# Seven block products per pair of heads in another order, with 21 between u and q and the banks exchanged from pair to pair

## The chip, the cores and the metric

One core of one Trainium2 chip runs the whole program in one launch. The metric is device time in microseconds (us), the median over the runs of a kernel; lower is better. The engines are called as the profile calls them: PE (matrix multiply), DVE (vector), ACT (scalar), POOL (GpSimd), SP (the queue that issues most transfers).

## What is computed

A decoder block on 512 tokens of width 2048, in float32. One projection gives the inputs of two groups of attention heads and their gates z:

```python
h = _rmsnorm(x, norm_g[l])
proj = h @ w_in[l]
(qa, kca, vca, ksa, vsa, kwa, vwa, za, ga,
 qb, kb, vb, zb) = jnp.split(proj, offsets, axis=-1)
...
y_a = o_a.reshape(B, S, WIDTH_A) * jax.nn.silu(za)   # 8 heads of 128: compressed, selected and window attention
...
y_b = o_b.reshape(B, S, WIDTH_B) * jax.nn.silu(zb)   # 16 heads of 64: window of 128 with sinks
x = x + jnp.concatenate([y_a, y_b], axis=-1) @ w_out[l]
return _rmsnorm(x, final_g)
```

Queries are turned by a rotary embedding (rope: products with a sine and a cosine table and a sum) before their scores.

## The kernel before

**Arithmetic.** A float32 factor is split into a high and a low word of a shorter format, and a product is the sum of three matmuls (`mm3`): L127 high·high, L128 high weight·low activation, L129 low weight·high activation. The splitting of a weight tile of 128 × 1024 is a *unit*: ACT copies the high word (L641, `whi`), DVE subtracts it from the raw tile (L642, `wlo`). The words lie in a pool of three buffers, so a unit can be built only when the product three units earlier has ended.

**A pair.** Heads go through the program one by one ("pairs" h = 1 to 14, the pair being a head's 128 columns of q and of z, where for group B one such head stands for two of the 64-wide ones). For a pair, q and z over the two halves of the tokens (H0 and H1, 256 columns each), summed over even and odd blocks of the inner dimension, form a 2 × 2 block product, done with seven products and sums before and after them (Strassen–Winograd). They have names:

- p (on the stored activation sums `pu00`, `pu10`), 22, 12, 21 and w on slices of the activations `xh`, `xl`, u on `pu01`, `pu11`, and q on further sums that lie in the rooms of `VH`, `VL`, `KH`, `KL`;
- each is 24 matmuls of 256 columns, so a pair has 168 and the fourteen have 98 products;
- weights come by `load` (SP, 512 KB each) from four quarters; the units of w, u and q are sums of quarters that DVE makes (L699, `raw`). Pairs h > 9 ("wide") have five buffers and let an accumulating transfer on POOL's queue make some of the sums.

The code is `pair` (from L681); the order of the products in it is 22, p, 21, 12, w, u, q. Two PSUM banks `pa`, `pb` (both named `pj`) take them by halves: `pa` holds p and 12 in its first half and w in its second; `pb` holds 22 and 21 in the first and u and q in the second. Between products DVE (`plus`, L699) and ACT (L731, L742, L747 and the like) carry the results to the rows of q (tile `t1`, shown as t; in wide pairs also `dd`) and of z (`zr`). When u has been read, q's rows are complete: the sine (L760, twice), the cosine (L761) on DVE, the sum on POOL (L762), then the split of the query.

**Attention.** Group A (`attn_a`, after each of the pairs h = 1 to 7 and once before) makes scores for four blocks of queries, "score sets" of 3, 6, 6 and 9 matmuls (L565) into one buffer `sp`, which DVE empties (L567, L571) before the next set; then exponentials on ACT, transposes on PE (L603, L615, L617) with their split (L533 on ACT, L534 on DVE), and the products with the values (L609 to L611, L624, L626). Group B (`attention`) runs in the following pair: scores S (L903, L904, two sets of 8 matmuls for each of the parts s0 and s1), transposes L936, values L942, L943, L948. Its query tile `qs` is put together by two ACT copies (L870), a DVE subtraction `qlo` (L873) and four transfers of 64 KB on SP's queue (L882).

**What sets the order.** The program is written as one stream; a scheduler with a model of the engines' times orders the instructions of each engine when the program is built, by priority in the order of the code and by readiness. The order on every engine is then fixed. For group B, `hooks` (L965 and following) says behind which product of the next pair a piece of attention is issued: s0 behind 21, s1 behind 12, k0 behind w, k2 and k3 behind u, k1 and the end behind q.

## Time and profile before

| | us |
|---|---|
| median of 3 runs | 834.11 (831.44 to 838.43) |
| the profiled execution | 830.96 |
| its span | 829.1 |
| PE busy in it | 796.3 (96%) |
| PE's weight loads (PEld) | 746.1 (90%) |
| DVE busy | 688.4 (83%) |
| ACT busy | 521.9 (63%) |
| POOL busy | 91.3 (11%) |
| mean granted clock of PE | 0.996 |

The pairs with attention A run from about 210 to 489 us, those with attention B from there to about 640; what precedes is the normalisation, the keys, values and compressed keys, what follows is head 15 and the output projection. A row of the timeline gives the start in us, the duration, the engine, the line, output<-inputs, and in brackets how long the engine stood idle before it and what ended that. A row of waits gives the engine with the waiting line and, behind the arrow, what ended the wait: the us in total, how often, the longest. A row of windows gives the stretch, its length, the busy time of PE, PEld, DVE, ACT and POOL with the count of instructions, the granted clock, the busy share of the transfer engines and GB/s.

### The profile page before, as it was taken

How to read it: one execution, taken by the hardware profiler on the slowest of the kernel's cores; microseconds unless marked ns; L12 is line 12 of the kernel's file. 1: busy time of each engine (PE TensorE's matmuls, PEld its weight loads, DVE VectorE, ACT ScalarE, POOL GpSimd, SP SyncE). 2: the span in 40 equal slices, each digit the busy share in tenths (PEclk: the TensorE clock that was granted, in tenths of full speed). 3: DMA queues.
4: the chain of work that ended last, by engine and by line, in shares of the span. 5: the costliest groups of instructions: out<-in, count | busy, mean ns of one | idle time of the engine just before them, and what ended most of it. 6: DMA issues, size and time to landing. Idle time of an engine off the chain costs nothing.

```text
span 829.1 us, 15441 instructions
## 1 busy us (share of the span) xinstructions
PE 796.3 (96%) x5782; PEld 746.1 (90%) x5782; DVE 688.4 (83%) x1283; ACT 521.9 (63%) x1088; POOL 91.3 (11%) x75
## 2 busy tenths in 40 slices
PE   8999999999999999999999999999999998899996
PEld 7788898988999999999999899899988887899996
DVE  6869785975798989997997898889987998678894
ACT  6734456662577867866777478676875657443545
POOL 3510002022010011010110012101110000100000
PEclk9999999999999999999999999999999999999999
DMA  8665886899712215323213585666674236697835
GB/s 308 210 204 166 277 283 209 250 307 359 251 44 95 77 42 165 109 61 113 85 58 115 159 205 153 168 174 153 179 261 158 77 102 245 189 262 192 267 66 203
DMA packets 60475, 145.03 MB, mean 175 GB/s; under 512 B 6257, under 2 KB 19825, under 8 KB 60401
## 3 DMA queue, kind: packets, MB, share of 16 engines
q1 hardware_dynamic: 56944, 132.00, 48.2%
q0 software_dynamic: 3168, 11.54, 8.2%
q8 instruction: 45, 0.74, 0.4%
q10 hardware_dynamic: 288, 0.52, 0.2%
q14 instruction: 30, 0.24, 0.1%
HBM read 121.65 MB, written 20.55 MB: 172 GB/s over the span
## 4 chain that ended last, share of the span: by engine, by line
PE 69%; DVE 10%; DMA 10%; ACT 4%; issue 4%; SPq 1%; POOL 1%; ACTq 0%; DVEq 0%; POOLq 0%
PE pj L127 12%; PE pj L129 12%; PE pj L128 12%; PE bank L129 4%; PE bank L128 3%; PE bank L127 3%; PE sp L565 3%; PE oa L128 3%; PE oa L129 3%; PE oa L127 3%; DMA rw<-wos 2%; DMA qs<-qlo 2%; DMA raw<-wq 1%; DVE wlo L642 1%; DMA ch<-wos 1%
## 5 line engine op out<-in xcount | busy, mean ns | idle before, releaser
L127 PE MATMUL pj<-xh,whi 128*128 128x256 f32 (+1 forms) x560 | 170.7, 305 | 2.7 <-ACT whi L641 1.5
L129 PE MATMUL pj<-xh,wlo 128*128 128x256 f32 (+1 forms) x560 | 170.1, 304 | 3.0 <-DVE wlo L642 2.9
L128 PE MATMUL pj<-xl,whi 128*128 128x256 f32 (+1 forms) x560 | 169.0, 302 | 0.0
L641 ACT ACTIVATE whi<-raw 128x1024 fp32r<-128x1024 f32 x98 | 102.8, 1054 | 46.7 <-PE pj L128 19.4
L642 DVE TENSOR_TENSOR wlo<-raw,whi 128x1024 fp32r<-128x1024 f32 x98 | 122.0, 1249 | 8.8 <-ACT whi L641 8.4
L129 PEld LDWEIGHTS pj<-xh,wlo 128*128 128x128 f32 x560 | 105.5, 188 | 8.9 <-DVE wlo L642 4.0
L127 PEld LDWEIGHTS pj<-xh,whi 128*128 128x128 f32 x560 | 105.5, 188 | 8.5 <-ACT whi L641 1.9
L128 PEld LDWEIGHTS pj<-xl,whi 128*128 128x128 f32 x560 | 105.4, 188 | 4.4 <-issue 0.2
L97 DVE TENSOR_TENSOR wlo<-raw,whi 128x512 fp32r<-128x512 f32 (+2 forms) x74 | 80.7, 1095 | 33.8 <-ACT whi L96 33.6
L96 ACT ACTIVATE whi<-raw 128x1024 fp32r<-128x1024 f32 (+1 forms) x73 | 65.3, 900 | 57.9 <-PE pj L128 14.9
L127 PE MATMUL pj<-pu,whi 128*128 128x256 f32 x224 | 63.9, 285 | 0.4 <-DVE zr L699 0.3
L129 PE MATMUL pj<-pu,wlo 128*128 128x256 f32 x224 | 63.4, 283 | 0.0
L128 PE MATMUL pj<-pu,whi 128*128 128x256 f32 x224 | 63.2, 282 | 0.0
L699 DVE TENSOR_TENSOR raw<-raw 128x1024 f32<-128x1024 f32 x46 | 58.0, 1261 | 0.2
L762 POOL TENSOR_TENSOR t<-t,t 128x512 f32<-128x512 f32 x14 | 24.4, 1745 | 248.1 <-DVE sums L584 79.6
L128 PE MATMUL oa<-wlo,xh 128*128 128x256 f32 (+1 forms) x168 | 50.3, 299 | 1.5 <-DVE wlo L1016 0.9
L127 PE MATMUL oa<-whi,xh 128*128 128x256 f32 (+1 forms) x168 | 50.0, 300 | 0.9 <-ACT whi L1015 0.9
L129 PE MATMUL oa<-whi,xl 128*128 128x256 f32 (+1 forms) x168 | 50.0, 299 | 0.0
L127 PEld LDWEIGHTS pj<-pu,whi 128*128 128x128 f32 x224 | 42.2, 189 | 1.4 <-DVE zr L699 1.3
L533 ACT ACTIVATE ph<-tp 128x512 fp32r<-128x512 f32 x56 | 32.1, 590 | 16.9 <-PE tp L936 8.6
L129 PEld LDWEIGHTS pj<-pu,wlo 128*128 128x128 f32 x224 | 42.3, 189 | 0.5 <-DVE wlo L642 0.2
L128 PEld LDWEIGHTS pj<-pu,whi 128*128 128x128 f32 x224 | 42.2, 188 | 0.1
(364 smaller groups left out, 2347.0 us busy)
## 6 DMA issues: line engine op xcount, KB each, us to landing
raw<-wq SPq DMA_DIRECT2D x65, 512.0 KB, 4.3
raw<-cw SPq DMA_DIRECT2D x16, 512.0 KB, 4.9
raw<-wos SPq DMA_DIRECT2D x12, 512.0 KB, 4.9
raw<-wq POOLq DMA_DIRECT2D x10, 512.0 KB, 5.6
rw<-wos SPq DMA_DIRECT2D x10, 512.0 KB, 5.7
xr<-xT SPq DMA_DIRECT2D x16, 256.0 KB, 5.3
raw<-w SPq DMA_DIRECT2D x8, 512.0 KB, 4.4
fd<-ft SPq DMA_DIRECT2D x4, 1024.0 KB, 5.8
```

The lines of the kernel that those rows point to most:

```text
L96: last["hi"] = act.activation(hi[:, :width], rw[:, :width], AF.Copy).ins
L97: last["lo"] = dve.tensor_tensor(out=lo[:, :width], in0=rw[:, :width], in1=hi[:, :width].bitcast(F32), op=ALU.subtract).ins
L127: pe.matmul(ps, ah, bh, start=first, stop=False, skip_group_check=go_on)
L128: pe.matmul(ps, ah, bl, start=False, stop=False, skip_group_check=go_on)
L129: recent["mm"] = pe.matmul(ps, al, bh, start=False, stop=last, skip_group_check=go_on).ins
L533: act.activation(ph, tp, AF.Copy)
L565: pe.matmul(sp[:, a:b], qq[:, qs], kk[0][:, ko:ko + b - a], start=pi == 0, stop=pi == 2)
L641: act.activation(hi, src, AF.Copy)
L642: last["lo"] = dve.tensor_tensor(out=lo, in0=src, in1=hi.bitcast(F32), op=ALU.subtract).ins
L699: return dve.tensor_tensor(out=out, in0=a, in1=b, op=op).ins
L762: pool.tensor_tensor(out=qv, in0=qv, in1=t2, op=ALU.add)
```

## The change

- The code order of the products becomes p, 22, 12, w, u, 21, q. d is now a copy of p from which 22 is subtracted; the signs of the later sums follow. The numbers of instructions on each engine stay the same.
- One bank, `pa`, takes p, 12, u and q in its first half and w in its second; `pb` takes 22 and 21 in its first half. Which of the two banks is `pa` alternates with h.
- The rotation of the weight buffers (`tags`) changes to match, the loads of quarter 0 and 3 change places at the start of a pair, quarter 1 (for 21) is asked for later in the code, and the accumulated load x4 of the wide pairs earlier. The first loads bring quarter 0 first.
- Lines shift: the sine is L755, the cosine L756 and the sum L757 after the change, and the copy of 12 is L742 (L747 before).
- The hooks are shifted: s0 behind 12, s1 behind w, k0 behind u, k2 and k3 behind 21, k1 and the end behind q.

```diff
--- before.py
+++ after.py
@@ -670,7 +670,7 @@
             for e in range(2):
                 nc.sync.dma_start(even[e][:, ms], source[e, :, ms])
 
-    tags = ["raw2", "raw0", "raw1", "raw3"]
+    tags = ["raw0", "raw2", "raw1", "raw3"]
 
     def load_quarter(src, tag, quarter):
         t = weights(tag)
@@ -698,13 +698,14 @@
         def plus(out, a, b, op=ALU.add):
             return dve.tensor_tensor(out=out, in0=a, in1=b, op=op).ins
 
+        c1, c2, c4, c3 = tags[:4]
         if wide:
-            c1, c2, c5, c3, c4 = tags
-            tags[:] = c4, c1, c2, c3, c5
+            c5 = tags[4]
+            tags[:] = c4, c2, c3, c5, c1
         else:
-            c1, c2, c4, c3 = tags
-            tags[:] = (c4, c1, c3, c2) if h < 9 else (c4, c1, "raw4", c3, c2)
-        pa, pb = [psp.tile([P, S], F32, name="pj", tag="pj") for e in range(2)]
+            tags[:] = (c1, c4, c3, c2) if h < 9 else (c1, c4, c3, c2, "raw4")
+        banks = [psp.tile([P, S], F32, name="pj", tag="pj") for e in range(2)]
+        pa, pb = banks if h % 2 else banks[::-1]
 
         def after(name):
             behind_mm((hooks or {}).get(name, ()))
@@ -714,12 +715,13 @@
         d, jj = qv[:, H1], zr[:, H0]
         if wide:
             d = wb.tile([P, 256], F32, name="dd", tag="dd")
+        x2 = load(c2, 0)
+        u3 = unit(x2)
         x1 = load(c1, 3)
         u0 = unit(x1)
-        x2 = load(c2, 0)
-        u3 = unit(x2)
         if wide:
             sm = load(c5, 0, 2)
+            x4 = load(c4, 2, 3)
         else:
             sm = x2
             x4 = load(c4, 2)
@@ -727,44 +729,42 @@
                 if "jj" in last:
                     behind.enter_context(tc.issue_after(last["jj"]))
                 plus(x2, x2, x4)
+        prod(pa[:, H0], u3, "p", True)
+        act.activation(d, pa[:, H0], AF.Copy)
         prod(pb[:, H0], u0, "22", True)
-        act.activation(d, pb[:, H0], AF.Copy, scale=-1.0)
-        x3 = load(c3, 1)
-        prod(pa[:, H0], u3, "p", True)
-        plus(d, d, pa[:, H0])
-        u2 = unit(x3)
-        prod(pb[:, H0], u2, "21", False)
-        act.activation(zr[:, H1], pb[:, H0], AF.Copy)
-        plus(jj, d, zr[:, H1])
-        after("21")
+        plus(d, d, pb[:, H0], ALU.subtract)
         u4 = unit(sm)
-        if wide:
-            x4 = load(c4, 2, 3)
-        else:
+        if not wide:
             plus(x4, x4, x1)
         plus(sm, sm, x1)
+        x3 = load(c3, 1)
         prod(pa[:, H0], u4, "12", False)
         act.activation(qv[:, H0], pa[:, H0], AF.Copy)
-        plus(jj, jj, qv[:, H0], ALU.subtract)
+        plus(jj, d, qv[:, H0], ALU.subtract)
         after("12")
         u1 = unit(x4)
         prod(pa[:, H1], u1, "w", True)
-        plus(d, d, pa[:, H1])
+        plus(qv[:, H1], d, pa[:, H1])
         after("w")
         u5 = unit(sm)
         plus(sm, sm, x3)
-        prod(pb[:, H1], u5, "u", True)
-        plus(qv[:, H1], d, pb[:, H1])
+        prod(pa[:, H0], u5, "u", True)
+        plus(qv[:, H1], qv[:, H1], pa[:, H0])
         t2 = wk.tile([P, S], F32, name="t2", tag="t2", bufs=1)
         for a, b in ((0, 64), (64, 0)):
             dve.tensor_tensor(out=t2[a:a + 64], in0=qv[b:b + 64], in1=sinA[b:b + 64], op=ALU.mult)
         dve.tensor_tensor(out=qv, in0=qv, in1=cosA, op=ALU.mult)
         pool.tensor_tensor(out=qv, in0=qv, in1=t2, op=ALU.add)
         qq = q_split(qv) if h < 8 else qb_split(qv)
+        after("u")
+        u2 = unit(x3)
+        prod(pb[:, H0], u2, "21", False)
+        act.activation(zr[:, H1], pb[:, H0], AF.Copy)
+        plus(jj, jj, zr[:, H1])
+        after("21")
         u6 = unit(sm)
-        after("u")
-        prod(pb[:, H1], u6, "q", False)
-        plus(jj, jj, pb[:, H1])
+        prod(pa[:, H0], u6, "q", False)
+        plus(jj, jj, pa[:, H0])
         after("q")
         last["jj"] = plus(zr, zr, rstdb, ALU.mult)
         st = wk.tile([P, S], F32, name="st", tag="st")
@@ -819,10 +819,10 @@
             lows, highs = slice(0, 4), slice(4, 8)
             first = []
             with tc.issue_after(last["dma"]):
-                first.append(load_quarter(wq[0], tags[0], 3))
+                first.append(load_quarter(wq[0], tags[1], 0))
                 forms_back(0, lows)
                 forms_back(1, lows)
-            for c, quarter in zip(tags[1:], (0, 2, 1)):
+            for c, quarter in ((tags[0], 3), (tags[2], 2), (tags[3], 1)):
                 with tc.issue_after(last["dma"]):
                     first.append(load_quarter(wq[0], c, quarter))
             with tc.issue_after(last["dma"]):
@@ -965,7 +965,7 @@
         hooks = {}
         if held:
             j, end, _ = held
-            hooks = {"21": [j["s0"]], "12": [j["s1"]], "w": [j["k0"]], "u": [j["k2"], j["k3"]], "q": [j["k1"], end]}
+            hooks = {"12": [j["s0"]], "w": [j["s1"]], "u": [j["k0"]], "21": [j["k2"], j["k3"]], "q": [j["k1"], end]}
         q2, st = pair(8 + i, (), hooks)
         if i == 0:
             back_b(0)
```

How the built order moves, at three places.

**PE, pair h = 5, behind product 12.** `sp_3841` and `sp_3854` are the score sets of the third and fourth block of queries, `pj` with `xh`, `xl` or `pu` a product. Before, the rows that follow the third set:

```order
L565 MATMUL sp_3841<-KH0_119,ql_3738 128x512
L610 MATMUL op_3371<-pl_3482,VH_1383 128x256 [waits DVE_49]
L611 MATMUL op_3371<-ph_3481,VL_1384 128x256
L609 MATMUL op_3371<-ph_3481,VH_1383 128x256
L610 MATMUL op_3371<-pl_3482,VH_1383 128x256
L611 MATMUL op_3371<-ph_3481,VL_1384 128x256
L609 MATMUL op_3371<-ph_3496,VH_1383 128x256 [waits Activation_49]
L610 MATMUL op_3371<-pl_3497,VH_1383 128x256 [waits DVE_49]
L611 MATMUL op_3371<-ph_3496,VL_1384 128x256
```

after which come the rest of these values, eight transposes, nine matmuls of product 12, eighteen of u and one of the values, and then the fourth set. Now the third set is followed by

```order
L565 MATMUL sp_3841<-KH0_119,ql_3708 128x512
L127 MATMUL pj_3939<-xh_108,whi_4008 128x256
L128 MATMUL pj_3939<-xl_109,whi_4008 128x256
L129 MATMUL pj_3939<-xh_108,wlo_4009 128x256
L565 MATMUL sp_3854<-KH0_119,qh_3707 128x288 [waits DVE_49,PE_49]
```

and behind the fourth set's last row stand

```order
L565 MATMUL sp_3854<-KH0_119,ql_3708 128x256
L127 MATMUL pj_3940<-xh_108,whi_4110 128x256 [waits Activation_49]
L128 MATMUL pj_3940<-xl_109,whi_4110 128x256
L127 MATMUL pj_3939<-xh_108,whi_4042 128x256 [waits Activation_49]
L128 MATMUL pj_3939<-xl_109,whi_4042 128x256
```

where `whi_4110` is the unit of 21 and `whi_4042` that of w. The values and transposes of the attention that stood between the two sets, and product u, are gone from there; three matmuls of 12 remain, then the fourth set, two matmuls of 21, and w.

**PE, pair h = 12, from u (`pu11`) to q (`VH`, first row with a wait on DVE).** Before, u's last rows are followed by w (`whi_6667`):

```order
L127 MATMUL pj_6472<-pu11_1364,whi_6710 128x256
L128 MATMUL pj_6472<-pu11_1364,whi_6710 128x256
L129 MATMUL pj_6472<-pu11_1364,wlo_6711 128x256
L127 MATMUL pj_6471<-xh_108,whi_6667 128x256 [waits Activation_49]
L128 MATMUL pj_6471<-xl_109,whi_6667 128x256
```

and q comes behind w, transposes and the next pair's 22 (`pj_6829`):

```order
L127 MATMUL pj_6829<-xh_108,whi_6835 128x256
L936 MATMUL tp_6697<-ident_61,ttb_6582 128x128 [waits Activation_49]
L127 MATMUL pj_6472<-VH_1383,whi_6755 128x256 [waits DVE_49]
L128 MATMUL pj_6472<-VL_1384,whi_6755 128x256
L936 MATMUL tp_6759<-ident_61,ttb_6638 128x128 [waits Activation_49]
L129 MATMUL pj_6472<-VH_1383,wlo_6756 128x256
```

Now:

```order
L129 MATMUL pj_6472<-pu11_1364,wlo_6667 128x256
L129 MATMUL pj_6471<-xh_108,wlo_6726 128x256
L127 MATMUL pj_6471<-xh_108,whi_6725 128x256
L128 MATMUL pj_6471<-xl_109,whi_6725 128x256
```

and after three more of 21

```order
L129 MATMUL pj_6471<-xh_108,wlo_6726 128x256
L936 MATMUL tp_6712<-ident_61,ttb_6578 128x128 [waits Activation_49]
L127 MATMUL pj_6472<-VH_1383,whi_6775 128x256 [waits DVE_49]
```

Here `whi_6725` is 21. Before, w and the first 22 of the 24 matmuls of the next pair's 22 stood between u and q; now seven matmuls of 21 and one transpose do, and most of 21 stands ahead of u.

**DVE, the same pair, from the read of u (`t1` out of `pj`) to `qlo`.** Before:

```order
L699 TENSOR_TENSOR t1_6473<-dd_6475,pj_6472 128x256
L956 TENSOR_TENSOR ob_6460<-opb_6339,ob_6460 64x512
L760 TENSOR_TENSOR t2_6740<-t1_6473,sinA_114 64x512 x2
L514 SCALAR_TENSOR_TENSOR st_6108<-ob_6460,st_6108 128x512
L761 TENSOR_TENSOR t1_6473<-t1_6473,cosA_113 128x512
L642 TENSOR_TENSOR wlo_6842<-raw_6839,whi_6841 128x1024
L534 TENSOR_TENSOR pl_6703<-tp_6697,ph_6702 128x512
L534 TENSOR_TENSOR pl_6765<-tp_6759,ph_6764 128x512
L873 TENSOR_TENSOR qlo_6749<-t1_6473,qs_6745 128x512
```

Now:

```order
L699 TENSOR_TENSOR t1_6473<-t1_6473,pj_6472 128x256
L514 SCALAR_TENSOR_TENSOR st_6108<-ob_6460,st_6108 128x512
L755 TENSOR_TENSOR t2_6696<-t1_6473,sinA_114 64x512 x2
L756 TENSOR_TENSOR t1_6473<-t1_6473,cosA_113 128x512
L917 TENSOR_TENSOR sums_6636<-sums_6636 128x4
L918 RECIPROCAL sums_6636<-sums_6636 128x4
L642 TENSOR_TENSOR wlo_6836<-raw_6833,whi_6835 128x1024
L642 TENSOR_TENSOR wlo_6842<-raw_6839,whi_6841 128x1024
L699 TENSOR_TENSOR zr_6474<-zr_6474 128x256
L699 TENSOR_TENSOR zr_6474<-zr_6474,pj_6472 128x256
L699 TENSOR_TENSOR zr_6474<-zr_6474,rstdb_68 128x512
L534 TENSOR_TENSOR pl_6718<-tp_6712,ph_6717 128x512
L642 TENSOR_TENSOR wlo_6902<-raw_6845,whi_6901 128x1024
L873 TENSOR_TENSOR qlo_6705<-t1_6473,qs_6701 128x512
```

The number of instructions between the two goes from eight to twelve: the units of the next pair's p, 22 and 12, the three sums of z and one split of a transpose stand there now.

## Prediction

> **What bounds the kernel now.** I read the page first, then the busy time by stage, then PE's waits, then the order of events around the pairs.
>
> ```profile
> span 829.1 us, 15441 instructions
> PE 796.3 (96%) x5782; PEld 746.1 (90%) x5782; DVE 688.4 (83%) x1283; ACT 521.9 (63%) x1088; POOL 91.3 (11%) x75
> 237.60:489.00 251.40, 243.60 (x2016) 237.71 (x2014) 223.47 (x474) 182.49 (x441) 23.80 (x17) 1.00 0.33 101
> 489.00:622.00 133.00, 127.27 (x1041) 122.21 (x1040) 117.27 (x255) 98.36 (x229) 19.03 (x13) 1.00 0.66 181
> 210.00:640.00 430.00, 416.48 (x3379) 402.52 (x3378) 377.55 (x806) 309.26 (x731) 44.59 (x31) 1.00 0.46 134
> ```
>
> PE sets the time. The fifth row is the stage of the fourteen pairs: 416.48 us of PE in 430.00, so PE stands for 13.5 us. That is the most that any reordering of this stage can give back, since the count of matmuls stays the same. The third row is the part with attention A (heads 0 to 7), the fourth the part with attention B; DVE is busy 89% and 88% of them, so whatever is put behind a DVE instruction there comes late. The granted clock is 1.00 (the third number from the end). What PE waits for in all:
>
> ```profile
> PE pj L129 <- DVE wlo L642: 2.9, 4, 0.9
> PE spb L903 <- DMA qs<-qlo: 2.5, 3, 1.2
> PE pj L127 <- ACT whi L641: 1.5, 2, 0.9
> PE op L609 <- ACT ph L533: 1.3, 2, 0.7
> PE op L609 <- ACT tt L593: 1.1, 1, 1.1
> PE pj L127 <- DVE t L699: 0.8, 2, 0.6
> PE pj L127 <- DVE dd L699: 0.6, 1, 0.6
> PE sp L565 <- DVE sums L571: 0.4, 1, 0.4
> PE pj L127 <- ACT t L731: 0.4, 1, 0.4
> PE pj L127 <- DVE zr L699: 0.3, 2, 0.2
> PE pj L127 <- ACT dd L731: 0.2, 1, 0.2
> ```
>
> Each row is a total, a count and the longest. No wait is longer than 1.2 us: PE always has another product or a piece of attention to go on with.
>
> **The change, part by part.** No arithmetic is added: 98 products of 24 matmuls and 98 units stay. What changes is which product can fill a wait.
>
> *q and the copies.* Product q no longer writes the half that DVE is reading as u, since most of 21 or the transposes stand between, and 21 gets a bank of its own beside 22. This can remove the rows "DVE t L699" (0.8), "ACT t L731" (0.4), "ACT dd L731" (0.2), "DVE dd L699" (0.6) and "DVE zr L699" (0.3): −2.3, and at worst 0.
>
> *The place behind product 12.* Now p, 12, w, u and q share a bank. w writes the other half than 12, yet in the changed order its first matmul carries a wait on ACT (the copy of 12), and u one on DVE (the read of w). Before, u lay in the other bank and ran there. 21 cannot fill the place: its unit takes the words slot of 12, so its copy can only begin when 12 has ended:
>
> ```profile
> L641 ACT ACTIVATE whi<-raw 128x1024 fp32r<-128x1024 f32 x98 | 102.8, 1054 | 46.7 <-PE pj L128 19.4
> L642 DVE TENSOR_TENSOR wlo<-raw,whi 128x1024 fp32r<-128x1024 f32 x98 | 122.0, 1249 | 8.8 <-ACT whi L641 8.4
> L747 ACT ACTIVATE t<-pj x14: 362/384/390, 222.1 to 605.3; 128x256 f32<-128x256 f32 x14
> ```
>
> The copy takes 1.05 us and the copy of 12 0.38. Only attention is left as cover. For heads 3, 5 and 7 that is two score sets with three matmuls of 12 between them, and the second set writes the buffer that DVE must first read out (one buffer). Before, some 40 matmuls stood there.
>
> ```profile
> 379.37 0.52 PE L565 MATMUL sp<-KH,ql 128*128 128x288 f32 x2
> 380.05 0.55 DVE L571 CUSTOM_DVE_ANT_0 tt<-sp,tab 128x384 f32<-128x384 f32 x1
> 381.00 0.08 DVE L571 DVE_READ_ACCUMULATOR2_ANT sums<- 128x1 f32 x1
> ...
> 280.93 0.19 DVE L567 CUSTOM_DVE_ANT_0 tc__2973<-sp,tab 128x32 f32<-128x32 f32 x1
> 285.75 0.08 DVE L571 DVE_READ_ACCUMULATOR2_ANT sums<- 128x1 f32 x1
> ...
> 380.08 0.28 PE L129 MATMUL pj<-pu,wlo 128*128 128x256 f32 x1
> 381.78 0.28 PE L129 MATMUL pj<-xh,wlo 128*128 128x256 f32 x1
> ```
>
> In the first three rows the set ends at 379.89 and DVE, which came at once, is done at 381.08: 1.19 us. In the next two DVE began at once as well (280.93) but did other work in between, and was done at 285.83, 4.9 us. The last two are the first and last of 16 matmuls: 0.113 us each. Three matmuls cover about 0.2 us of the wait, so PE stands 1.0 to 4.7 us. In the changed order DVE's five instructions of this set stand behind one another with no unit between, so I stay near the lower end: 1.4 each, 4.2 for three heads. For heads 4, 6, 8 and 9 one set of six to eight matmuls, about 1.0 us, and two matmuls of 21 are the cover, 1.25. On ACT the copy of 21's unit and the copy of 12 follow on 12's end: 0.28 (the last matmul) + 1.05 + 0.38 = 1.71, 0.46 too much and 0.1 less, since the words come free one matmul earlier. So the stall is 0.35 with ACT free and 1.4 with another copy of 1.05 ahead; ACT is busy 73% of this stage (182.49 of 251.40), mostly with shorter instructions, and I take 0.6, 2.4 for four. Heads 2 and 10 to 14 have ten or more attention matmuls there, and in head 1 w stands ahead of 21 and needs the copy of 12 alone, 0.66 under a cover of 1.07: nothing. Together **+6.6**, between 0 (if the attention covers it all) and 20 (3 × 4.7 + 4 × 1.4).
>
> [...]
>
> *The way of q to the scores of B.* From DVE's read of u the head goes over the rope, the copies, DVE's qlo (L873) and four small transfers to the first score matmul (L903).
>
> ```profile
> 505.96 0.42 DVE L699 TENSOR_TENSOR t<-dd,pj 128x256 f32<-128x256 f32 x1 [0.99 <-PE pj L129]
> 506.42 1.39 DVE L760 TENSOR_TENSOR t<-t,sinA 64x512 f32<-64x512 f32 x2
> 508.52 0.67 DVE L761 TENSOR_TENSOR t<-t,cosA 128x512 f32<-128x512 f32 x1
> 509.12 0.16 DVE L918 RECIPROCAL sums<-sums 128x4 f32<-128x4 f32 x1
> 509.21 2.32 DVE L642 TENSOR_TENSOR wlo<-raw,whi 128x1024 fp32r<-128x1024 f32 x2
> 511.45 0.40 DVE L699 TENSOR_TENSOR zr<-zr,pj 128x256 f32<-128x256 f32 x1
> 511.78 0.68 DVE L534 TENSOR_TENSOR pl<-tp,ph 128x512 fp32r<-128x512 f32 x1
> 513.20 0.69 DVE L699 TENSOR_TENSOR zr<-zr,rstdb 128x512 f32<-128x512 f32 x1
> 514.95 0.69 DVE L514 SCALAR_TENSOR_TENSOR st<-ob,st 128x512 f32<-128x512 f32 x1
> 515.55 0.69 DVE L873 TENSOR_TENSOR qlo<-t,qs 128x512 fp32r<-128x512 f32 x1
> 516.30 3.31 SPq L882 DMA_DIRECT2D qs<-qlo  x4
> 520.87 0.65 PE L948 MATMUL opb<-pd,vb 128*64 128x128 f32 x4
> 522.72 0.36 PE L903 MATMUL spb<-VH,qs 128*128 128x256 f32 x1 [1.20 <-DMA qs<-qlo]
> DMA to landing us min/median/max: 1.9/3.3/5.8
> ```
>
> In this pair of before, PE reached the scores 15.6 us after the read of u (521.52) and waited 1.20. In the changed order PE has about 118 matmuls on the way, 118 × 0.113 = 13.3 and the attention's wider ones: 13.6 to 14.2. On DVE stand read 0.42, L514 0.69, sine 1.39, cosine 0.67, two small ones 0.2, the units of p' and 22' 2.32, three zr instructions 0.40 + 0.40 + 0.69, L534 0.68, the unit of 12' 1.22 (half of 2.32, or 1.25 by the row of L642), qlo 0.69: 9.8 us without a wait. From qlo's end, issue and landing bring the last quarter after 3.9 (2.0 of issues before the last, 1.9) to 6.5 (here: 516.24 to 522.72). On SP's queue the four transfers stand behind the store L516 and one weight load in both orders, so the queue adds nothing new. The data is there at 13.7 to 16.3 against PE's 13.9: a stall of 0 to 2.4. I take 1.2, near the one of this row, in five pairs (heads 10 to 14): 6.0, less the 2.5 that before has: **+3.5**, between −2.5 and +9.5.
>
> *Units behind u in B.* DVE's read, L514, sine, cosine, the two small ones and the first unit are 4.6 us, while PE has about 37 matmuls, 4.25: 0.3 in five pairs, 1.5 against 0.9 in one of the four waits on wlo before: **+0.6**, between −0.9 and +2.
>
> *What the stalls give back.* While PE stands 6.6 us longer in stage A, DVE and ACT go on; the four first rows of waits without L903 come to 6.8, of which 0.9 are charged above. A third of the rest: **−2.0**, between 0 and −5.9.
>
> *Free.* The first load now brings quarter 0 for p first; its data and the sums that 22 needs are there long before PE is done with what precedes the pairs, by the order of issues; x4's accumulated load is issued earlier in the wide pairs, on queues that are not waited for there. If that cover is gone, a unit is late by one landing, 4.3 us.
>
> Sum: 6.6 + 3.5 + 0.6 − 2.3 − 2.0 = +6.4. The profiled execution took 830.96 (span 829.1), 3.15 less than the median 834.11, so I forecast 837.4 for such an execution and **840.5** for the median.
>
> **The rivals.** *It does not do what it says* (0.19): the scheduler takes the first matmuls of 21 ahead of w and most of the rest ahead of u, so that only 3 to 7 remain between u and q. If these two moves cover the place behind 12 as u did, only single waits are exchanged: 0 to +1, 834 to 835. For it: no wait of before is above 1.2. Against: 21's unit cannot be ready when 12 ends.
>
> *Slower* (0.33): the scores of B wait for the qs transfers, place L903 in heads 11 to the last. At the upper end, 2.7 a pair (with 0.3 of DVE's waits), it is 13.5 − 2.5 = 11.0 instead of 3.5: +13.9, 848.0. From 1.6 a pair (2.0 us more in five pairs) it decides that the time is over 1% longer, 842.5. For it: the shortest path on DVE, 9.8, already has no slack with the median landing of 3.3 behind 2.0 of issues. Against: before, two of the three waits there were short.
>
> *Faster* (0.09): the place behind 12 stays covered, because ACT and DVE are ahead of PE there, and the quarters land in time: 0 − 2.5 + 0.6 − 2.3 − 2.0 = −6.2, 827.9. Against: DVE at 89%. The whole of PE's idle time bounds it at −13.5, 820.6.
>
> **How the numbers follow.** Forecast 0.39, no effect 0.19, slower 0.33, faster 0.09. The likeliest gives 840.5; its own range is 837 to 844. A measurement of this kernel tells about 1% (8.3 us) from no change. Over 1% slower: nearly all of the slower case (0.31) and a sixth of the forecast (0.06), 0.37. Over 1% faster: two thirds of the faster case, 0.06. Within 1%: 0.57. The range reaches down to 829 (most of the faster case outside) and up to 851, 3 us above the slower case for the upper prices behind 12.
>
> **What would show it.** Right: rows of PE waiting in L565 for DVE's L571 with more than 3 us in all, about 1 to 2 us in heads 3, 5, 7; waits of pj on ACT's copies, of 12 and of 21's unit, in heads 4, 6, 8, 9; L903 waiting for qs in four or five pairs, 4 to 8 us in all; no wait on "DVE t L699" at q; PE's idle time in the stage of the pairs up from 13.5 to about 20. Wrong: L565 waits under 1 us in all (then the term behind 12 fails), L903 waits under 2.5 (then the way of q does), or a new wait on raw weights.

## The result and the profile after

The changed kernel takes 844.70 us (median of 4 runs, 843.97 to 844.75) against 834.00 for the kernel before (831.44 to 838.43). The ratio is 1.013, 95% interval 1.0098 to 1.0163: it is slower. The time lies 4.2 above the 840.5 that was forecast and inside the range. The profiled execution took 844.74.

The page of the changed kernel, and below it one row of windows for each kernel, from the first score matmul of attention A to the first matmul of the output projection (before, then after; length, then busy PE, then the others, and the granted clock third from the end):

```profile
span 843.0 us, 15406 instructions
PE 802.8 (95%) x5782; PEld 752.2 (89%) x5782; DVE 698.8 (83%) x1283; ACT 522.0 (62%) x1088; POOL 90.6 (11%) x75
```

```profile
210.23:656.41 446.18, 432.02 (x3465) 415.52 (x3463) 393.43 (x857) 317.93 (x754) 44.59 (x31) 1.00 0.45 132
```

```profile
208.18:670.34 462.16, 438.55 (x3468) 420.94 (x3466) 401.45 (x856) 317.72 (x756) 44.32 (x31) 0.99 0.43 127
```

The whole loss lies in this stretch: it grew by 15.98 us. What comes before is 2.05 shorter and what follows equal (172.69 and 172.66), though the changed kernel has one stretch at half the clock there (at 719.17) and the kernel before has none. PE stands 462.16 − 438.55 = 23.61 us instead of 14.16, 9.45 more. But it is also *busy* 6.53 us longer with the same matmuls, and the clock is not 1.00: those are two different losses. The first one, in PE's waits in this stretch (the longest rows):

```profile
PE sp L565 <- DVE sums L571: 9.2, 6, 2.0
PE sp L565 <- DVE sums L584: 4.3, 3, 1.4
PE pj L127 <- ACT zr L762: 3.0, 3, 1.1
...
PE spb L903 <- DMA qs<-qlo: 2.2, 2, 2.0
...
PE opb L942 <- ACT ph L533: 1.4, 1, 1.4
...
PE pj L127 <- ACT whi L641: 0.9, 1, 0.9
...
PE pj L129 <- DVE wlo L642: 0.6, 3, 0.3
```

L565 are the score sets of attention A, which waited 0.4 us in one place before and now wait 13.5 in nine: in heads 1 (2.03), 2 (0.92 and 0.60), 3, 5 and 7 (1.44, 1.42, 1.42) and 4, 6 and 8 (1.93, 1.81, 1.93). Head 5 is the place that the prediction worked out, three matmuls of 12 between two sets. PE:

```profile
348.20 0.52 PE L565 MATMUL sp<-KH,ql 128*128 128x288 f32 x2
348.79 0.28 PE L129 MATMUL pj<-xh,wlo 128*128 128x256 f32 x1
350.50 0.72 PE L565 MATMUL sp<-KH,qh 128*128 128x288 f32 x3 [1.42 <-DVE sums L584]
```

Head 4 is a place that it did not see: ten matmuls of 12 (the first from 312.58) stand between the second and the third set, and when the second set ends DVE still has a unit and L514 to do before it reads the set. PE, then DVE:

```profile
312.37 0.36 PE L565 MATMUL sp<-KH,ql 128*128 128x256 f32 x1
...
313.64 0.28 PE L129 MATMUL pj<-xh,wlo 128*128 128x256 f32 x1
315.85 0.60 PE L565 MATMUL sp<-KH,qh 128*128 128x288 f32 x2 [1.93 <-DVE sums L571]
```

```profile
313.09 1.22 DVE L642 TENSOR_TENSOR wlo<-raw,whi 128x1024 fp32r<-128x1024 f32 x1
314.22 0.68 DVE L514 SCALAR_TENSOR_TENSOR st<-op,st 128x512 f32<-128x512 f32 x1
314.82 0.18 DVE L567 CUSTOM_DVE_ANT_0 tc__3372<-sp,tab 128x32 f32<-128x32 f32 x1
...
315.62 0.08 DVE L571 DVE_READ_ACCUMULATOR2_ANT sums<- 128x1 f32 x1
```

The second loss is the clock. The trace shows five lowered stretches while PE works, at 316.40, 381.25, 609.95, 664.56 and 719.17 us. Each lasts 3.41 us at a clock of 0.50, and the distances between their starts are 19, 67, 16 and 16 times 3.41. So I cut the time into pieces of 3.41 us that end where such a stretch begins. The changed kernel around the stall of head 4, and around that of head 8:

```profile
309.57:312.98 3.41, 3.41 (x32) 3.41 (x31) 3.32 (x5) 1.55 (x5) 0.00 (x0) 1.00 0.14 14
312.98:316.40 3.42, 1.49 (x11) 1.27 (x11) 3.42 (x10) 2.51 (x8) 0.00 (x0) 1.00 0.75 281
316.40:319.81 3.41, 3.41 (x16) 3.22 (x15) 3.34 (x12) 1.40 (x7) 0.00 (x0) 0.50 0.47 126
319.81:323.22 3.41, 3.41 (x32) 3.41 (x31) 0.91 (x3) 1.94 (x5) 0.00 (x0) 1.00 0.31 123
...
442.69:446.10 3.41, 2.10 (x19) 1.90 (x17) 3.38 (x7) 2.25 (x4) 0.00 (x0) 1.00 0.65 187
446.10:449.52 3.42, 2.80 (x20) 2.71 (x21) 3.42 (x10) 1.47 (x7) 0.00 (x0) 1.00 0.50 196
449.52:452.93 3.41, 3.41 (x31) 3.41 (x30) 2.35 (x9) 3.35 (x11) 0.00 (x0) 1.00 0.44 154
```

Both stalls are 1.93 us. The first lies whole in one piece: PE is busy 1.49 of 3.41, and for the next piece the clock is 0.50 and PE does 16 matmuls instead of 32. The second falls across a border (2.10 and 2.80 busy), and the clock stays at 1.00. The stage has four such lowered stretches, behind the stalls that end at 315.85, 381.05, 609.29 and 664.20 (1.93, 1.81, 1.96 and 1.38 us); each loses half of 3.41, 1.71 us, 6.8 in all, close to the 6.53 of longer busy time. The kernel before has none there in its profiled execution. The length of a stall alone does not tell which piece loses the clock: the fourth stall is only 1.38 us, and the longest one, 2.03 us before 219.25, of which 1.84 lie in one piece, cost nothing more.

### The profile page after: what moved, and what is told of

It is laid out like the page before. It is cut to its first block, busy times and chain, and to the rows that moved or that the text cites. A ratio compares the mean times of both kernels' runs of the same rounds, so it can differ in the third digit from the quotient of the medians.

```text
span 843.0 us, 15406 instructions
## 1 busy us (share of the span) xinstructions
PE 802.8 (95%) x5782; PEld 752.2 (89%) x5782; DVE 698.8 (83%) x1283; ACT 522.0 (62%) x1088; POOL 90.6 (11%) x75
## 4 chain that ended last, share of the span: by engine, by line
PE 51%; DVE 25%; DMA 11%; issue 6%; ACT 5%; SPq 1%; POOL 0%; DVEq 0%; ACTq 0%; POOLq 0%
PE pj L127 7%; PE pj L128 7%; PE pj L129 7%; DVE wlo L642 6%; PE bank L129 4%; PE bank L127 4%; PE bank L128 4%; PE oa L128 3%; PE oa L129 3%; PE oa L127 3%; DVE raw L699 2%; PE sp L565 2%; DMA rw<-wos 2%; DVE zr L699 2%; DVE tt L571 1%
## 5 line engine op out<-in xcount | busy, mean ns | idle before, releaser
L127 PE MATMUL pj<-xh,whi 128*128 128x256 f32 (+1 forms) x560 | 171.1, 306 | 1.7 <-ACT whi L641 0.9
L128 PE MATMUL pj<-xl,whi 128*128 128x256 f32 (+1 forms) x560 | 169.9, 304 | 0.0
L642 DVE TENSOR_TENSOR wlo<-raw,whi 128x1024 fp32r<-128x1024 f32 x98 | 128.7, 1323 | 10.4 <-ACT whi L641 9.8
L127 PEld LDWEIGHTS pj<-xh,whi 128*128 128x128 f32 x560 | 106.9, 191 | 7.2 <-ACT whi L641 1.3
L128 PEld LDWEIGHTS pj<-xl,whi 128*128 128x128 f32 x560 | 106.6, 190 | 4.6
L127 PE MATMUL pj<-pu,whi 128*128 128x256 f32 x224 | 64.3, 287 | 2.2 <-ACT zr L762 2.2
L128 PE MATMUL pj<-pu,whi 128*128 128x256 f32 x224 | 62.6, 280 | 0.0
L699 DVE TENSOR_TENSOR raw<-raw 128x1024 f32<-128x1024 f32 x46 | 57.1, 1241 | 0.2
L757 POOL TENSOR_TENSOR t<-t,t 128x512 f32<-128x512 f32 x14 | 24.9, 1781 | 278.7 <-DVE t L756 197.7
L127 PE MATMUL oa<-whi,xh 128*128 128x256 f32 (+1 forms) x168 | 50.1, 300 | 1.1 <-ACT whi L1015 0.9
L128 PE MATMUL oa<-wlo,xh 128*128 128x256 f32 (+1 forms) x168 | 50.4, 300 | 0.6 <-DVE wlo L1267 0.6
L127 PEld LDWEIGHTS pj<-pu,whi 128*128 128x128 f32 x224 | 42.2, 189 | 3.2 <-ACT zr L762 2.9
L128 PEld LDWEIGHTS pj<-pu,whi 128*128 128x128 f32 x224 | 42.2, 188 | 0.0
```

The lines of the kernel that those rows point to most:

```text
L127: pe.matmul(ps, ah, bh, start=first, stop=False, skip_group_check=go_on)
L128: pe.matmul(ps, ah, bl, start=False, stop=False, skip_group_check=go_on)
L642: last["lo"] = dve.tensor_tensor(out=lo, in0=src, in1=hi.bitcast(F32), op=ALU.subtract).ins
L699: return dve.tensor_tensor(out=out, in0=a, in1=b, op=op).ins
L757: pool.tensor_tensor(out=qv, in0=qv, in1=t2, op=ALU.add)
```

## The experiments

My theory is that the new order and the shared bank together leave nothing ready behind product 12, so that score sets run into one another, and that a stall of about 1.8 us or more costs another 1.7 by the clock (an estimate from the three of 1.93, 1.81 and 1.96 us above). The rivals: the order alone is at fault, or the bank alone, the hooks are, or the clock is a condition of the chip in those runs.

One remark ahead, on the built programs: built without the exchange of the two banks from pair to pair, the lists of instructions of all engines are the same, and product p of each pair gets the same bank: the pool gives a pair's first product the bank that comes free first. The exchange changes names only.

### One part at a time

**Order alone.** u and q go back to the other bank; the rest of the change stays. (In this kernel u opens the second half of the bank between 22 and 21, which were to add up in the first half, and the kernel leaves that sum out; the instructions and their sizes are as with it.)

```diff
-        pa, pb = banks if h % 2 else banks[::-1]
+        pa, pb = banks
...
-        prod(pa[:, H0], u5, "u", True)
-        plus(qv[:, H1], qv[:, H1], pa[:, H0])
+        prod(pb[:, H1], u5, "u", True)
+        plus(qv[:, H1], qv[:, H1], pb[:, H1])
...
-        prod(pa[:, H0], u6, "q", False)
-        plus(jj, jj, pa[:, H0])
+        prod(pb[:, H1], u6, "q", False)
+        plus(jj, jj, pb[:, H1])
```

Expected: 

> The changed kernel with only u and q taken back to the other half of the bank of 22 and 21; the product order, hooks and loads of the change stay. My theory: the loss sits where attention's score sets follow one another with 3 or 10 matmuls between them, since w and u share a bank with 12 and nothing else is ready; here the least cover in the built order is 22 matmuls from the second set of a head on, so the waits of L565 fall from 13.5 us to under 4, the granted clock returns to 0.993 or more, and 0.3 to 1 us per head is paid anew where 21 waits for the read of u: 834 to 840. Rival (the order itself, 21 between u and q, or the later hooks cost the time): 842 to 847, with the L565 waits wherever they are. Rival (the lower clock belongs to the chip's condition in those runs and not to the kernel): a clock of 0.986 to 0.988 here too.

Measured: 827.52 us (9 runs, 824.36 to 829.53), ratio 0.9933 (0.9903 to 0.9962). No L565 wait is left, and no lowered stretch in the stage. The order by itself is not the cause, and the time is below the range that I gave.

**Banks alone.** The kernel before with u and q in the bank of p, 12 and w, the old order and hooks:

```diff
-        prod(pb[:, H1], u5, "u", True)
-        plus(qv[:, H1], d, pb[:, H1])
+        prod(pa[:, H0], u5, "u", True)
+        plus(qv[:, H1], d, pa[:, H0])
...
-        prod(pb[:, H1], u6, "q", False)
-        plus(jj, jj, pb[:, H1])
+        prod(pa[:, H0], u6, "q", False)
+        plus(jj, jj, pa[:, H0])
```

Expected: 

> The kernel before with only u and q moved to the first half of the bank of p, 12 and w, and the exchange of names from pair to pair; the old product order and hooks stay. My theory: sharing a bank costs by itself, because w and u follow each other through ACT's and DVE's reads, but 21 ahead of 12 leaves 21's unit out of the way: two score sets with 4 and 5 matmuls of cover remain in the built order (1.5 us each) and some waits of u on the read of w: 836 to 841. Rival (the order alone costs): within 1% of 834 and PE waits as before.

Measured: 826.55 us (6 runs, 824.59 to 829.16), ratio 0.9917 (0.9881 to 0.9952). I was wrong in the sign: sharing the bank in the old order gains. Its cost is there (w waits for the copy of 12, L748, u for the read of w, L699) and the score sets wait little:

```profile
PE pj L127 <- ACT t L748: 3.4, 6, 1.0
PE pj L127 <- DVE dd L699: 3.0, 5, 0.9
...
PE sp L565 <- DVE sums L571: 1.6, 2, 0.8
```

So each half of the change is worth −0.7 to −0.8% and both together +1.3%: the loss is in neither, but in the two together.

**Hooks earlier.** The changed kernel with s0 behind 22, s1 behind 12, k0 behind w, k2 and k3 behind u:

```diff
-            hooks = {"12": [j["s0"]], "w": [j["s1"]], "u": [j["k0"]], "21": [j["k2"], j["k3"]], "q": [j["k1"], end]}
+            hooks = {"22": [j["s0"]], "12": [j["s1"]], "w": [j["k0"]], "u": [j["k2"], j["k3"]], "q": [j["k1"], end]}
```

Expected: 

> The changed kernel with the attention pieces of heads 8 to 14 hooked one product earlier (behind 22, 12, w, u, q). My theory: stage A is not touched, so its 13.5 us of L565 waits stay; in stage B the scores are reached about 2.8 us earlier than the four qs transfers land, 1 to 3 us of wait in each of five pairs: 846 to 856. Rival (the later hooks are what made the change slow): 834 to 840.

Measured: 847.72 us (4 runs), ratio 1.0164 (1.0122 to 1.0206). L565 still waits 13.4 us, the scores 3.4 instead of 2.2 for the transfers (in two places, not in five). The later hooks were not the cause of the loss.

### The clock by itself

The trace of the changed kernel gives what the theory starts from: lowered stretches of 3.41 us at 0.50, whole multiples of 3.41 apart, and in the 3.41 us ahead of the first of them 1.92 us in which PE stands (3.41 less 1.49), a little over half.

Expected: 

> A small kernel of its own that computes nothing of the block: trains of 120 matmuls of 256 columns on PE, and between them a pause in which DVE reads the bank 1, 2, 3, 4 or 5 times (128 x 512 each, about 0.65 us), nine times each. My theory on the clock: time is cut in fixed windows of 3.41 us, and a window in which PE stands for more than about half is followed by one at half the clock. Then pauses of 1 or 2 reads (0.7, 1.3 us) never lower the clock, 3 reads (2.0 us) only where the pause lies whole in one window, 4 and 5 reads (2.6, 3.3 us) in most cases, and each lowered stretch is 3.41 us and costs 1.7 us. Rival (the clock falls for reasons of the chip): lowered stretches have no relation to the length of the pause ahead of them, or there are none.

This kernel computes nothing of the block: PE's trains depend on DVE's reads of their bank, and that is all.

```python
for g in GAPS:
    for k in range(g):
        dve.tensor_copy(ev, bank)
    train(TRAIN)
```

The pauses came out as 0.78, 1.51, 2.23, 2.96 and 3.68 us. Two pauses of 2.96 us, at 84.95 to 87.91 and at 170.87 to 173.83, in pieces of 3.41 us by the same borders:

```profile
83.18:86.60 3.42, 1.77 (x15) 1.57 (x14) 1.54 (x3) 0.00 (x0) 0.00 (x0) 1.00 0.02 5
86.60:90.01 3.41, 2.10 (x17) 2.10 (x18) 1.22 (x2) 0.00 (x0) 0.00 (x0) 1.00 0.00 0
90.01:93.42 3.41, 3.41 (x31) 3.41 (x30) 0.00 (x0) 0.00 (x0) 0.00 (x0) 1.00 0.00 0
...
168.52:171.93 3.41, 2.35 (x20) 2.15 (x18) 0.98 (x2) 0.00 (x0) 0.00 (x0) 1.00 0.00 0
171.93:175.34 3.41, 1.51 (x12) 1.51 (x13) 1.78 (x3) 0.00 (x0) 0.00 (x0) 1.00 0.00 0
175.34:178.75 3.41, 3.41 (x18) 3.41 (x17) 0.00 (x0) 0.00 (x0) 0.00 (x0) 0.50 0.02 5
```

The same pause cost nothing more where the border divided it (1.65 and 1.31 us of standing) and was followed by a stretch at 0.50 where 1.90 us fell into one piece. Over the 45 pauses: none of the 31 with at most 1.75 us of standing in any one piece was followed by a lowered clock, and all 14 with 1.9 or more were: one of the nine of 2.23 us, four of the nine of 2.96, all nine of 3.68, and none of 0.78 and 1.51. Where a pause of 3.68 went on into the lowered stretch, the stretch lasted two pieces (6.83 us). The mean granted clock of the run is 0.958. In this kernel the clock followed PE's standing in these 45 pauses and not a condition of the chip.

### Where 21 stands

If the fault is that 21's words take the slot of 12, then 21 one, two or three products earlier should cure it, with the banks of the change. In each, the block of 21 moves (shown for the place between w and u), and the hooks keep their places by number; ahead of 12 the load of quarter 1 moves with it.

```diff
+        u2 = unit(x3)
+        prod(pb[:, H0], u2, "21", False)
+        act.activation(zr[:, H1], pb[:, H0], AF.Copy)
+        plus(jj, jj, zr[:, H1])
+        after("21")
...
         prod(pa[:, H0], u5, "u", True)
...
-        u2 = unit(x3)
-        prod(pb[:, H0], u2, "21", False)
-        act.activation(zr[:, H1], pb[:, H0], AF.Copy)
-        plus(jj, jj, zr[:, H1])
-        after("21")
```

**Between w and u.** Expected: 

> The changed kernel with 21 one product earlier, between w and u (order p, 22, 12, w, 21, u, q), banks as in the change; the attention pieces stay at the same places by number. The only thing this gives back is that 21's words take the slot of 22 instead of that of 12, so 21 is ready when 12 ends. My theory (order and shared bank together leave nothing ready behind 12, and the score sets run into each other): the least cover of a second to fourth score set in the built order rises from 3 to 10 in head 3 and 26 or more elsewhere; L565 waits from 13.5 us to under 4, no lowered clock in the stage with attention A, 826 to 834. Rival (the shared bank under the new order costs, through w and u waiting for the reads): within 1% of 844.

Measured: 845.20 us (4 runs), ratio 1.0131 (1.0101 to 1.0162). My range failed by over 11 us, though its first step held: L565 waits 0.5 us instead of 13.5. PE now stands elsewhere:

```profile
PE pj L129 <- DVE wlo L642: 8.6, 8, 1.5
PE spb L903 <- DMA qs<-qlo: 5.9, 2, 3.8
...
PE pj L127 <- ACT whi L641: 2.9, 1, 2.9
...
PE sp L565 <- DVE sums L571: 0.5, 2, 0.3
```

The first row is product 12, not 21: by the order of the built program PE begins it (L127, L128) and then stands for its low words, in eight heads. Why DVE makes them later here than in the changed kernel (where all waits on L642 came to 0.6) was not tried. No stretch is lowered in the stage with attention A now, but four pieces are in the stage with B. That one set of waits vanishes says nothing on the time, when the order behind it is thin elsewhere.

**Between 12 and w.** Expected: 

> The same with 21 two products earlier, between 12 and w (order p, 22, 12, 21, w, u, q). My theory: as the run with 21 ahead of u, 826 to 834, with waits of w on the copy of 12 gone as 21 stands between, and instead u and q on the reads of w and u, 0.5 to 0.9 us each in some heads. Rival (the shared bank): 838 to 845.

Measured: 821.66 us (4 runs, 819.97 to 823.78), ratio 0.9843 (0.9811 to 0.9875), below my range and below both kernels. 21 covers the copy of 12 and w covers 21's; u still waits 1.9 us for the read of w, in four places. L565 waits 1.5 us, L642 1.5, and no stretch of the stage is lowered.

**Ahead of 12.** Expected: 

> The same with 21 three products earlier, ahead of 12 as in the kernel before (order p, 22, 21, 12, w, u, q), but with the banks and the first product p of the change. My theory: as the run that changed the banks alone, 824 to 830, since only p and 22 are exchanged against it. Rival (the first product matters: p first waits for the copy of 21): 832 or more with waits of p on ACT.

Measured: 839.41 us (5 runs), ratio 1.0062 (1.0038 to 1.0086). Wrong again, by ten us, and not by the rival's wait either (p does not wait for ACT):

```profile
PE pj L127 <- DVE t L699: 7.1, 9, 1.7
PE pj L129 <- DVE wlo L642: 4.3, 4, 2.2
...
PE pj L127 <- ACT t L747: 2.2, 2, 2.0
```

Here u follows w with few or no attention matmuls between, in one bank, and waits for DVE's read nine times. Against the run that changed the banks alone, p and 22 are exchanged and the weights come as in the change; which of these puts w and u side by side was not tried.

L565 waits little in all three (0.5, 1.5 and no row), so the place of 21 does make those waits. But only one of the three places cures the time: in the other two PE stands elsewhere, and the slot of 21's words is not shown to be the whole fault.

### Hooks later

Edit, here on the run that changed the banks alone; in the others the names differ with the order, the places are the same:

```diff
-            hooks = {"21": [j["s0"]], "12": [j["s1"]], "w": [j["k0"]], "u": [j["k2"], j["k3"]], "q": [j["k1"], end]}
+            hooks = {"12": [j["s0"]], "w": [j["s1"]], "u": [j["k0"], j["k2"]], "q": [j["k3"], j["k1"], end]}
```

**On the banks alone.** Expected: 

> The run that changed the banks alone (826.55), with the attention pieces of heads 8 to 14 hooked one product later (s0 behind 12, s1 behind w, k0 and k2 behind u, k3, k1 and the end behind q). My theory: there the scores wait 2.3 us for the qs transfers, which falls to about 0, and nothing else is short of cover: 823 to 827. Rival (later pieces run into the next pair's): waits on L936 and on the copies of the transposes rise by more than 2.3, 828 to 832.

Measured: 818.94 us (4 runs, 815.93 to 822.34), ratio 0.9811 (0.9773 to 0.9848): the lowest median of all, and 4 us below my range. The stage with attention B is 207.85 us instead of 214.54. The scores' wait fell as expected, from 2.3 to 0.3. What I had not expected: w's wait for the copy of 12 (3.4 us in the run before it) and u's for the read of w (3.0) went with it:

```profile
PE sp L565 <- DVE sums L571: 1.7, 2, 0.9
...
PE pj L127 <- ACT t L748: 0.4, 2, 0.2
PE spb L904 <- DMA qs<-qlo: 0.3, 1, 0.3
PE pj L127 <- DVE dd L699: 0.2, 1, 0.2
```

**On the kernel before.** Expected: 

> The kernel before with only the attention pieces of heads 8 to 14 hooked later (s0 behind 12, s1 behind w, k0 and k2 behind u, k3, k1 and the end behind q). My theory: the scores then no longer wait for the qs transfers (2.5 us) and the values no longer for ACT; as in the pair of runs 826.55 and 818.94, most of 9.2 us of idle time in the stage with attention B goes: 825 to 830. Rival (the gain came from the banks as well): 831 to 836.

Measured: 833.09 us (10 runs, 827.74 to 839.87), ratio 0.9997 (0.9965 to 1.0029): no effect, the rival was right. In its profiled execution the scores' wait fell from 2.5 to 1.8, and that for the low words (L642) rose from 2.9 to 5.9; that execution, at 839.87, is the slowest of the ten.

**On the run with 21 between 12 and w.** Expected: 

> The run with 21 between 12 and w (821.66) with the attention pieces of heads 8 to 14 one product later (s0 behind 21, s1 behind w, k0 and k2 behind u, k3, k1 and the end behind q). My theory: 6.0 us of idle time in the stage with attention B falls to 3 to 4: 817 to 821. Rival: later pieces collide with the next pair, 822 to 826.

Measured: 821.41 us (4 runs), ratio 0.9863 (0.9818 to 0.9908), the same as without (821.66), so no gain; PE's standing in the stage with B went from 6.0 to 5.9 us only. The scores' wait for the transfers rose, from 0.9 to 4.2 us, since in three pairs the last quarter of `qs` landed 6 to 7.5 us after the end of `qlo` instead of 3.9.

**On the changed kernel.** Expected: 

> The changed kernel with the attention pieces of heads 8 to 14 one product later still (s0 behind w, s1 behind u, k0 and k2 behind 21, k3, k1 and the end behind q). My theory: the waits of the scores for the qs transfers (2.2 us) and the lowered clock behind the longest of them (1.7) go, stage A keeps its 13.8 us: 836 to 842. Rival (the pieces are already late): 844 to 850.

Measured: 854.92 us (4 runs), ratio 1.0244 (1.02 to 1.0289). The wait for the transfers went, and in its place the values wait for DVE:

```profile
PE opb L943 <- DVE pl L534: 6.8, 5, 2.1
PE pj L127 <- ACT whi L641: 5.0, 6, 1.9
```

So where the hooks should stand can't be told without the order of the products; my forecast for them had the right direction in one of four runs.

### Work added instead of waiting

```diff
         prod(pa[:, H0], u4, "12", False)
+        if 3 <= h <= 8:
+            with tc.issue_after(recent["mm"]):
+                for m in range(10):
+                    pe.matmul(pb[:, H1], u4[0][:, 0:P], xf["12", 0][0], start=False, stop=True, skip_group_check=True)
```

Expected: 

> The changed kernel with ten more matmuls of 256 columns behind product 12 of heads 3 to 8, 60 in all, which write a half of a bank that nobody reads: pure extra work of 60 x 0.113 = 6.8 us. In the built order they stand between the score sets, and w moves ahead of the later sets: the least cover of a second to fourth set in these heads rises from 3 to 23 matmuls. My theory: the L565 waits fall from 13.5 us to under 4, the two lowered stretches of the stage with attention A go, so the kernel gets faster by added work: 13.8 of idle time to 5, + 6.8, - 3.4, that is 834 to 841. Rival (PE's idle time there is not what costs, or moves elsewhere as in the run with 21 ahead of u): 846 to 853.

Measured: 840.13 us (6 runs, 839.02 to 843.88), ratio 1.0089 (1.006 to 1.0119): 6.8 us of idle work more than the changed kernel, and not slower than it. The waits of L565 in heads 3 to 8 are gone; the 3.7 that remain are those of heads 1 and 2:

```profile
PE sp L565 <- DVE sums L571: 3.7, 3, 2.2
...
PE pj L129 <- DVE wlo L642: 2.9, 5, 1.5
```

But the stage with attention A is 248.12 us against 245.96: the added work took the place of the waits there and did not beat them, and it has two lowered stretches as before, behind other stalls (217.84 and 342.03). That the profiled execution is 4.5 us shorter all the same comes from outside this stage: 3.0 in the stage with B, which has one lowered stretch fewer, 2.2 at the end and 1.5 ahead of the pairs. So the time fell into my range, but not by the way that I had given. The run shows that cover takes away the waits of L565, and not that covering them pays more than the work it takes.

### All kernels on one line

For the stretch from the first score matmul to the output projection, in the profiled executions: its length, PE's time not busy in it (length less busy, from a row of windows as above), the lowered stretches in it at 1.71 us each, and what is left. Each row is one execution; that of "before, hooks later" is the slowest of its ten (839.87, median 833.09).

| kernel | length | PE not busy | lowered stretches | rest |
|---|---|---|---|---|
| before | 446.2 | 14.2 | 0 | 432.0 |
| changed | 462.2 | 23.6 | 4 = 6.8 | 431.7 |
| order alone | 445.6 | 11.9 | 0 | 433.7 |
| banks alone | 443.4 | 13.3 | 0 | 430.1 |
| hooks earlier | 466.2 | 27.0 | 4 = 6.8 | 432.4 |
| 21 between w and u | 462.4 | 24.5 | 4 = 6.8 | 431.0 |
| 21 between 12 and w | 441.0 | 10.5 | 0 | 430.5 |
| 21 ahead of 12 | 459.0 | 21.0 | 1 = 1.7 | 436.3 |
| banks, hooks later | 437.0 | 7.6 | 0 | 429.4 |
| added work (less 6.8) | 454.6 | 17.6 | 3 = 5.1 | 431.9 |
| before, hooks later | 455.6 | 20.2 | 3 = 5.1 | 430.3 |
| 21 between 12 and w, hooks later | 440.5 | 9.4 | 0 | 431.1 |
| changed, hooks later | 470.6 | 31.2 | 4 = 6.8 | 432.6 |

The rest is 429 to 434 in twelve of thirteen, and 436 with 21 ahead of 12. It holds short delays too: a row of PE lasts 0.28 us while matmuls of a train start every 0.117, so a delay below some 0.16 us is counted as busy. Counted from start to start, outside the lowered stretches, the starts that come over 0.06 us later than the median of their form add 16 to 20 us in the twelve and 23 with 21 ahead of 12; less that, 412 to 414 are left in all thirteen. The time of this stage is the work, plus PE's standing and short delays, plus the clock; the changed kernel's +16.0 is 9.4 + 6.8, within 0.3.

## Why the prediction was right and where it was wrong

The direction, the place and the first mechanism were right; the forecast of 840.5 was 4.2 short, and the chances put most on "within 1%". That it was not further off is in part luck: for the profiled execution the forecast was 837.4 and 844.74 came, 7.3 more, and 3.5 us that did not come (the way of q) stand against 3.0 that were not foreseen (p and the copy of 21). By its steps, with the predicted and the measured change in PE's time:

- **The place behind 12, heads 3, 5 and 7**: 4.2 predicted, 1.44 + 1.42 + 1.42 = 4.3 measured, nearly as worked out: three matmuls were the cover, and in head 5 DVE came 0.5 us after the end of the set (349.24 after 348.72), with no unit between.
- **Heads 4, 6, 8 and 9**: 2.4 predicted, 5.7 + 0.9 measured (0.9 by ACT in head 9). The step took the waits for ACT behind the set as the price; but in heads 4, 6 and 8 the set itself waits, because only ten matmuls separate it from the one before it. The waits of pj for ACT that were named as a sign for these four heads came in one. The order of the changed program showed this; I had read the rows behind 12 and not those ahead of its last ten matmuls.
- **Heads 1 and 2**: nothing predicted, 2.03 + 0.92 + 0.60 = 3.6 measured, the same wait with 15 to 72 matmuls of cover in the built order and DVE later still. The term behind 12 as a whole was 6.6 and came out at 13.1 of L565 waits (13.5 less 0.4) and 0.9 of ACT.
- **What the stalls give back**: −2.0 predicted. In stage A all waits other than L565 fell from 4.4 to 0.3 us: −4.1. That ACT and DVE get ahead while PE stands is not shown to be the whole reason: with the order alone, where no set waits, these waits are 3.1.
- **q and the copies**: −2.3 predicted, and all five rows are gone; q still stands 0.25 us twice, at 541.02 and 593.73, just behind DVE's read of u. In exchange, and not foreseen, the bank of 22 and 21 goes to p of the next pair (behind the last pair, to head 15's first product), which waits for ACT's copy of 21, and this copy stands behind two units: 3.0 us in three places. ACT, then PE:

```profile
515.71 1.99 ACT L641 ACTIVATE whi<-raw 128x1024 fp32r<-128x1024 f32 x2
517.72 0.38 ACT L762 ACTIVATE zr<-pj 128x256 f32<-128x256 f32 x1
```

```profile
518.16 0.38 PE L127 MATMUL pj<-pu,whi 128*128 128x256 f32 x1 [1.10 <-ACT zr L762]
```

- **The way of q to the scores**: +3.5 predicted, −0.3 measured (2.2 in two places against 2.5), so by the prediction's own sign, under 2.5, this step failed. DVE's part was nearly right (qlo ends 10.0 to 10.8 us after the start of the read of u in heads 9 to 14, for 9.8 worked out), but the transfers landed sooner, 3.9 us after qlo's end in four of these six pairs, the lower bound, and in three pairs PE came later by waits of its own (1.10 in the rows above). Why the transfers were sooner was not tried. The summary of L882's line, whose median landing was 3.3 before:

```profile
DMA to landing us min/median/max: 1.9/2.0/5.8
```

- **Units behind u**: +0.6 predicted, −0.4 measured (0.17 + 0.15 in stage B against 0.77 at 510.45 before; the 0.9 that the prediction set against it is a wait at 305.73, in stage A).
- **The clock**: not in the prediction, which read "The granted clock is 1.00" and let a stall cost its own length. It measured +6.8. This is the step that failed most: "no wait of before is above 1.2" was read as a sign that waits are small; they also went with a clock of 1.00 and no lowered stretch in that stage (210.23 to 656.41).

In the stage that makes +9.4 and +6.8 against a forecast of +6.4. The profiled execution differs by 13.8 only, since the one of before has a lowered stretch at 130 us, ahead of the pairs, and took 2 us more there; the medians differ by 10.7, since that execution was 3.0 below its median. It also has a high clock for its kernel: 0.996, while 38 other executions of the kernel before on record have 0.988 to 0.996, median 0.993, and the four of the changed kernel 0.986 to 0.988. So the clock's share of the difference between medians is less than in the profiles; from these means I estimate 5.6 us over the whole run (0.0135 × 843 less 0.007 × 832), against 7.6 in the profiles (0.0127 × 843 less 0.0037 × 829).

Whether w could write one half of a bank while the other half is read is not shown here. The built program waits in either half, and in the run with the banks alone these waits come to 3.4 us behind the copy of 12; no run lets w write while the other half is read.

## What to carry to other kernels

Where an order is fixed ahead and PE sets the time, a change of order is read from the rows: for each buffer that is written anew only after it was read out, count the matmuls between its writer and its next writer, over the whole stage and not only at the place of the edit. Two changes that gain alone can lose together, when each uses up the spare product that covers the other, and a wait that is removed shows nothing until PE's whole standing is added up. And a stall can have a price beyond its length: in the changed kernel the 1.93 us before 315.85, all in one piece of 3.41 us, cost another 1.71 by the clock, and the 1.93 us of head 8, which a border divided, did not. By that a stall of 1.9 us would be better split in two, which no run here tried; filling it with idle work did not pay in the one run that did.

## What the hardware showed that I had not expected

In the changed kernel stalls of PE of 1.93, 1.81 and 1.96 us were each followed by 3.41 us at a clock of 0.50; another of 1.93 us, which a border between two pieces of 3.41 us divided, was not. The same stall of 1.93 us cost 1.9 or 3.6 us, by where it lay among the pieces. In the small kernel all 45 pauses followed this, with the border between 1.75 and 1.9 us of standing in one piece.

In the block's kernels PE's busy time marked the border less sharply. Two pieces of the changed kernel, of which the first lost the clock and the second kept it:

```profile
661.15:664.56 3.41, 1.88 (x13) 1.30 (x11) 1.58 (x7) 1.64 (x3) 0.00 (x0) 1.00 0.38 128
217.41:220.83 3.42, 1.58 (x13) 1.61 (x14) 2.24 (x9) 1.90 (x5) 0.00 (x0) 1.00 0.79 222
```

By PE they are in the wrong order (1.88 and 1.58), by the weight loads, the next number, in the right one (1.30 and 1.61). Over all pieces of the thirteen kernels, PE busy up to 2.29 us lost the clock and down to 1.58 kept it; with weight loads, up to 1.68 lost it and down to 1.44 kept it; in the kernel before, the piece from 126.69 lost it with 2.11 and 1.57 and the one from 703.54 kept it with 1.58 and 1.58. So the weight loads tell it better, and neither exactly; why was not tried.
